# Low parts of weights made by an accumulating load, and four of eight row pairs as seven products, in the last stage of a decoder trunk

## The chip, the cores and the metric

The kernel runs on one core of one Trainium2 chip. The metric is the device time of one execution in microseconds (us). The core has a matrix engine (TensorE, PE in the profile), an elementwise vector engine (VectorE, DVE), an activation engine (ScalarE, ACT), GpSimd (POOL) and SyncE (SP), which here issues all the transfers of the kernel before. Sixteen DMA engines carry the transfers.

## The reference

The program is a decoder trunk of two layers on 256 tokens of width 2048, all in float32. Layer 0 mixes tokens by retention, layer 1 by a gated short convolution; each layer ends with a SwiGLU feed-forward part of inner width 5632, and a final RMS norm closes the trunk. What the change touches is the feed-forward part of layer 1 and the norm behind it:

```python
def swiglu(h, w_in, w_out):
    a, b = jnp.split(h @ w_in, 2, axis=-1)
    return (jax.nn.silu(a) * b) @ w_out
...
        h = (rms_norm(x, norm2_g[i]) * (1.0 + sc2) + sh2).astype(x.dtype)
        x = (x + g2 * swiglu(h, ffn_w_in[i], ffn_w_out[i])).astype(x.dtype)
    return rms_norm(x, final_g).astype(x.dtype)
```

## The kernel before, in words

**Products in two parts.** Each float32 operand is held as a high part, rounded to the matrix engine's float32r type, and a low part, what is left (`lo = raw - hi`). A product of two operands is three matmuls: high by high, high by low, low by high (`thrice`, L460 to L462). The second of the three is the first that needs the low part of the weights.

**Weights.** All weights lie in one array `w_all` in the order of their use, in blocks of 128 x 2048 (1 MB). SP loads a block into a `raw` buffer (three of them, L372). A block is cut into pieces of 1024 columns, or 512. For each piece ACT makes `hi` (L402) and DVE makes `lo` (L405). There are four `hi` and four `lo` buffers (`PART_BUFS`), used in rotation: a piece can be written only when PE is done with the piece four places ahead of it. In the last stage three pieces are prepared ahead of the one in use.

**The last stage.** It is the feed-forward part of layer 1, in two halves (20 and 24 tiles of the inner width). Its first matrix is worked off in ten groups (4 in the first half, 6 in the second), each for four inner tiles; a group goes over eight blocks, 0 to 7, of one pair of row tiles each. The second matrix follows each half in two groups, four in all, of 10 or 12 pairs; the last of them ends with six tiles of rows taken column by column.

**Common blocks and Sevens.** A common block has two pieces, here called b.0 and b.1 for block b, each of four products: 24 matmuls of 512 columns. For some pairs (`IN_SEVEN` of the first matrix, `OUT_SEVEN` of the second) the 2 x 2 blocks of tokens, rows and columns are multiplied with seven products in place of eight (a Strassen-Winograd scheme, class `Seven`): 21 matmuls. Such a block has four pieces, b.2 to b.5, of two, two, two and one product. DVE works more for it: the differences of weight blocks (L391, 1024 columns, into one buffer shown as `x`, since it lies in an old part of x), two further ones in place in `raw` (L395 and L397, 512 columns each), and the low parts of 3.5 times 1024 columns. In place of a common block's two low parts these are four instructions of 1024 columns and three of 512. The sums of tokens that the scheme needs on the other side are made once for the first matrix (`made_in_sums`) and per pair for the second (`tokens_sums_of`, L1142 to L1145).

**At the end of a group.** When the last Seven of a group is done, four banks are combined (`mixed_sums`: ACT's copy L1240, then DVE's L1241 to L1244), and after block 7 the sums are added (L1315, DVE), followed by silu (L1319, ACT) and a product (L1320, DVE). The transposes of this result back to rows (`turned`: PE L1329, ACT L1332 and L1333, DVE L1334) are taken up two blocks into the next group (`TURNS_AT`).

**What sets the order.** PE's order is that of the code. The orders of ACT, DVE, POOL and SP are set at build time by a scheduler, and each engine works through its own list strictly in order: an instruction that waits holds up all behind it.

Of the kernel before, what the change touches and what calls it, by code (L numbers as in the profile page):

```python
# [10 lines left out]
F32 = mybir.dt.float32  # L11
F32R = mybir.dt.float32r
I32 = mybir.dt.int32
AF = mybir.ActivationFunctionType
ALU = mybir.AluOpType
PSUM = bass.MemoryType.PSUM

P = 128
# [14 lines left out]
HALF = 1024  # L33
# [4 lines left out]
LEAD = 6  # L38
ROOTS_AT, SPREAD_AT = 1, 3
TAIL_ROWS = 6  # L40
IN_SEVEN, OUT_SEVEN, TURNS_AT, BESIDE_CB, BESIDE_SUMS = (3, 5), (2, 4, 6), 2, 40, 48
LAST_TILES = 20, 24
STORE_AT, LOAD_AT = 0, 2
LEAD_RET, LEAD_CONV, LEAD_FFN = 6, 4, 2
# [97 lines left out]
class Seven:  # L142
# [6 lines left out]
    n = 2 * DV // P  # L149
# [12 lines left out]
def in_pairs(cols, rows, sevens):  # L162

    return [Seven(cols, r) if i in sevens else Group(cols, DV, ks=r) for i, r in rows]
# [13 lines left out]
def last_out(part):  # L178

    first, n = part * LAST_TILES[0], LAST_TILES[part]  # L180
    order = list(range(n // 2))
    if not part:
        a, b = order[-2:]
        order = order[:5] + [a, order[6], b, order[5], order[7]]
    rows = [(i, [first + 2 * i, first + 2 * i + 1]) for i in order]
    out = []
    for c in range(0, D, 2 * DV):
        cols, rest = [c, c + DV], 0
        if part and c + 2 * DV == D:
            rest = TAIL_ROWS // 2  # L190
        out.append(in_pairs(cols, rows[: len(rows) - rest], OUT_SEVEN))
        if rest:
            out[-1] += [Group([col], DV, ks=[k for _, r in rows[-rest:] for k in r]) for col in cols]
    return out
# [62 lines left out]
def trunk(ctx: ExitStack, tc: tile.TileContext, x_in, c_in, pos_in, w_mod, cols_in, gain_in, tab_in, w_all, out):  # L257
    nc = tc.nc
# [11 lines left out]
    def tmp(tag, shape=(P, S), dtype=F32, pool=work, bufs=None):  # L270
        return pool.tile(list(shape), dtype, tag=tag, name=name(tag), bufs=bufs)
# [11 lines left out]
    cols = const.tile([P, n_cols], F32, tag="cols", name="cols")  # L283
# [78 lines left out]
    in_seven, n = set(), 0  # L362
    for g in groups:
        if isinstance(g, Seven):
            in_seven.add(n // CHUNK)
        n += g.n * P * len(g.ks)

    pieces = [(i, p) for i in range(w_all.shape[0]) for p in ((2, 3, 4, 5) if i in in_seven else (0, 1))]

    def fetch():  # L370
        raw = wpool.tile([P, CHUNK], F32, tag="raw", name=name("raw"), bufs=RAW_BUFS)
# [4 lines left out]
    def prepare(between=None):  # L376
        if prepared[0] == len(pieces):
            return
        _, piece = pieces[prepared[0]]
        prepared[0] += 1  # L380
        if piece in (0, 2):
            if not fetched:
                fetch()
            raws[:] = [fetched.pop(0)]
            while first <= units[0] < early and len(fetched) < RAW_BUFS - 1 and n_fetched[0] < w_all.shape[0]:
                fetch()
        whole = raws[0]
        b = [whole[:, i : i + DV] for i in range(0, CHUNK, DV)]
        raw = whole[:, :HALF] if piece in (0, 4) else whole[:, HALF:]
        if piece == 2:  # L390
            nc.vector.tensor_tensor(differences, whole[:, DV : 3 * DV], whole[:, : 2 * DV], op=ALU.subtract)  # L391
        elif piece == 3:
            raw = differences
        elif piece == 4:
            nc.vector.tensor_tensor(b[1], b[2], differences[:, :DV], op=ALU.subtract)  # L395
        elif piece == 5:
            nc.vector.tensor_tensor(b[3], b[3], b[1], op=ALU.subtract)  # L397
            raw = b[3]
        width = raw.shape[1]
        hi = wpool.tile([P, HALF], F32R, tag="hi", name=name("hi"))[:, :width]  # L400
        lo = wpool.tile([P, HALF], F32R, tag="lo", name=name("lo"))[:, :width]
        nc.scalar.copy(hi, raw)  # L402
        if between:
            between()
        nc.vector.tensor_tensor(lo, raw, hi.bitcast(F32), op=ALU.subtract)  # L405
        ready.append((hi, lo, width))

    prepared, ahead_now = [0], [AHEAD]
# [270 lines left out]
    with ExitStack() as inner:  # L679
# [64 lines left out]
        with tc.tile_pool(name="start", bufs=1) as sp:  # L744
# [132 lines left out]
            due, step = [], [0.0]  # L877
# [245 lines left out]
    def turn(t, c):  # L1123
# [8 lines left out]
    needed(1, GT2)  # L1132
    in_cb = const.tile([P, D], F32R, tag="cb", name="in_cb")
    tokens_sums = [
        v.rearrange("p (i n) -> p i n", i=2) for v in (in_cb[:, : 6 * P], in_cb[:, 6 * P : 12 * P])
    ] + [mpool.tile([P, 2, 3 * P], F32R, tag="sums_of_tokens", name="sums_of_tokens")]

    def tokens_sums_of(a11, a21, a12, a22, third, others):

# [11 lines left out]
    def parts(both):  # L1151

        return [both[:, i, t * P : (t + 1) * P] for i in range(2) for t in range(2)]

    in_sums = {}

    def made_in_sums():

        tmp("beside_sums", (P, BESIDE_SUMS), bufs=1)
        for i in IN_SEVEN:  # L1160
            both = tmp("u512", (P, 2, S), pool=mpool, bufs=3)
            for n in range(2):
                k = 2 * i + n
                high, low = [h[k].bitcast(F32)[:, v, :] for v in range(2)]
                nc.vector.tensor_tensor(both[:, n, :], high, low, op=ALU.add)
            tag = "low" if in_sums else "u"
            in_sums[i] = [tmp(tag, (P, 2, P), F32R, bufs=3) for _ in range(3)]
            tokens_sums_of(*parts(both), h[2 * i][:, :, P:], in_sums[i])

    def three(v):  # L1170
        return [v[:, :, n * P : (n + 1) * P] for n in range(3)]

    turns = [lambda t=t, c=c: turn(t, c) for c in range(4) for t in range(2)]

# [136 lines left out]
    def last_input(groups, pairs, seven):  # L1311

        ours, extra = gathered(groups, h, 0, in_sums)
        for (t, j), pt in ours.items():
            nc.vector.tensor_tensor(extra[t, j], pt, extra[t, j], op=ALU.add)  # L1315
        ms = []
        for t in range(2):
            m = extra[t, 0]
            nc.scalar.activation(m, m, AF.Silu)  # L1319
            nc.vector.tensor_tensor(m, m, extra[t, 1], op=ALU.mult)  # L1320
            ms.append(m)

        def turned():
            for n, (dst, of) in enumerate(zip(pairs, seven)):
                pt = bank()
                for i in range(2):
                    for t, m in enumerate(ms):
                        c = slice((2 * n + i) * P, (2 * n + i + 1) * P)
                        nc.tensor.transpose(pt[:, i, t * P : (t + 1) * P], m[:, c], ident)  # L1329
                if of is not None:  # L1330
                    both = tmp("u512", (P, 2, S), pool=mpool, bufs=3)
                    nc.scalar.copy(both, pt)  # L1332
                nc.scalar.copy(dst[:, :, 0, :], pt)  # L1333
                nc.vector.tensor_tensor(dst[:, :, 1, :], pt, dst[:, :, 0, :].bitcast(F32), op=ALU.subtract)  # L1334
                if of is not None:
                    tokens_sums_of(*parts(both), dst[:, 0, :, P:], [of])

        waiting.append(turned)

    def last_output(part, c, groups, act, base):  # L1340

        final = part and c

        def beside(i):
            if not part and not c and i == STORE_AT:
                gate_stored()
            if not part and not c and i == LOAD_AT:
                spread()
            if part and not c and i == LOAD_AT:
                last_gain = hpool.tile([P, D], F32, tag="h", name="last_gain")  # L1350
                nc.sync.dma_start(last_gain, gain_in.broadcast_to([P, D]))
                gain_of.extend(at(last_gain, v) for v in range(4))

        def mixed(extra):
            for (t, j), v in extra.items():
                gated(t, c + j, v, 0)

        sums = {i: three(v) for i, v in zip(OUT_SEVEN, tokens_sums)}
        ours, extra = gathered(groups, act, base, sums, beside, mixed if final else None)
        if final:  # L1360
            return
        for (t, j), pt in ours.items():
            nc.vector.tensor_tensor(extra[t, j], pt, extra[t, j], op=ALU.add)
        for (t, j), v in extra.items():
            gated(t, c + j, v, MOD_PRIO)
            if part:
                xs, n = at(xt[t], c + j), c + j
                nc.scalar.activation(v, xs, AF.Square, accum_out=total[:, t, n : n + 1])
                nc.vector.tensor_tensor(xs, xs, gain_of[n], op=ALU.mult)
# [16 lines left out]
    for part in range(2):  # L1386
        n = LAST_TILES[part] // 2
        mid = mids(LAST_TILES[part]) if part else first_mid
        if not part:
            first_rows(mid[-2:])  # L1390
            made_in_sums()
            ahead_now[0] = AHEAD + 1
        for i, groups in enumerate(LAST_IN[part]):
            seven = [tokens_sums[OUT_SEVEN.index(q)] if q in OUT_SEVEN else None for q in (2 * i, 2 * i + 1)]
            last_input(groups, mid[2 * i : 2 * i + 2], seven)
        act = [mid[k // 2][:, k % 2] for k in range(2 * n)]
        for c, groups in enumerate(LAST_OUT[part]):
            last_output(part, 2 * c, groups, act, part * LAST_TILES[0])
# [37 lines left out]
```

## Time and profile before

| | |
|---|---|
| time, median of three runs | 2597.03 us (2595.98 to 2597.09) |
| the profiled execution | 2600.71 us, of which the span is 2598.8 us |
| PE busy | 2567.0 us, 99% of the span |
| DVE busy | 2157.4 us, 83% |
| ACT busy | 1289.4 us, 50% |
| POOL busy | 125.7 us, 5%; in the last stage next to nothing |
| loads of weights, in the whole program | 456 of 1 MB |
| mean DMA rate | 265 GB/s |
| granted TensorE clock | 0.999 |

Busy time on PE counts each matmul until its end, and matmuls overlap: one of 512 columns is listed with 390 ns, while the next starts about 227 ns after it. So the pitch from start to start is what a matmul costs on a PE that never waits. DVE's and ACT's instructions overlap a little in the same manner. "Idle before" with an arrow names what an engine waited for just before an instruction.

### The profile page before, as it was taken

The page shows a single profiled execution, that of the slowest core. Times are in us where ns is not written, and L with a number is a line of the kernel's source. Part 1 is how long each engine was busy: PE and PEld are TensorE (multiplying, and loading weights), DVE is VectorE, ACT ScalarE, POOL GpSimd, SP SyncE. Part 2 cuts the span into 40 slices and gives each one's busy share as a digit, 9 for nine tenths or more (in the row PEclk, how much of TensorE's full clock was granted, in tenths as well). Part 3 has the DMA queues.
Part 4 walks back from the last instruction along what each step waited for, and adds up shares of the span by engine and source line. Part 5 has one row for each costly group of instructions (what it writes and reads, how often), then busy time and mean ns, then how long its engine had stood idle before and what let it go on. Part 6 is the DMA issues. An engine that isn't in the chain of part 4 may idle for free.

```text
span 2598.8 us, 36365 instructions
## 1 busy us (share of the span) xinstructions
PE 2567.0 (99%) x14211; PEld 2241.0 (86%) x14211; DVE 2157.4 (83%) x2702; ACT 1289.4 (50%) x1768; POOL 125.7 (5%) x232
## 2 busy tenths in 40 slices
PE   7999999999999999999999999999999999999998
PEld 6898889888889888888888898888998888888886
DVE  7988978887698887777777889988988888888877
ACT  5544543444456454334444454444565554555554
POOL 0000000110000000100001001000000000000000
PEclk9999999999999999999999999999999999999999
DMA  9975668877676888787778868877845565554653
GB/s 399 387 290 221 255 246 300 299 261 276 244 284 247 330 325 305 298 299 302 294 284 296 299 237 313 326 290 277 305 171 204 190 217 203 184 207 182 221 200 146
DMA packets 96686, 689.55 MB, mean 265 GB/s; under 512 B 10737, under 2 KB 12161, under 8 KB 13441
## 3 DMA queue, kind: packets, MB, share of 16 engines
q1 hardware_dynamic: 96514, 687.23, 71.1%
q8 instruction: 111, 1.82, 0.3%
q14 instruction: 61, 0.50, 0.1%
HBM read 685.08 MB, written 2.11 MB: 264 GB/s over the span
## 4 chain that ended last, share of the span: by engine, by line
PE 84%; DVE 7%; DMA 5%; issue 2%; ACT 1%; ACTq 0%; POOLq 0%; POOL 0%; DVEq 0%; SPq 0%
PE bank L447 25%; PE bank L450 14%; PE bank L461 12%; PE bank L460 12%; PE bank L462 12%; DMA raw<-w_all 4%; DVE lo L405 3%; DMA raw<-w_mod 2%; PE bank L496 2%; PE bank L495 1%; PE bank L494 1%; PE bank L627 1%; PE bank L629 1%; PE bank L628 1%; DVE raw L755 1%
## 5 line engine op out<-in xcount | busy, mean ns | idle before, releaser
L402 ACT CAST hi<-raw 128x1024 fp32r<-128x1024 f32 (+1 forms) x944 | 973.1, 1039 | 1037.0 <-PE bank L462 385.6
L405 DVE TENSOR_TENSOR lo<-raw,hi 128x1024 fp32r<-128x1024 f32 (+1 forms) x944 | 1129.9, 1203 | 347.4 <-ACT hi L402 340.0
L447 PE MATMUL bank<-h,hi 128*128 128x512 f32 x2016 | 699.2, 390 | 0.0
L450 PE MATMUL bank<-h,lo 128*128 128x256 f32 x2016 | 568.4, 282 | 0.0
L447 PEld LDWEIGHTS bank<-h,hi 128*128 128x128 f32 x2016 | 378.3, 188 | 79.2
L460 PE MATMUL bank<-hi,h 128*128 128x512 f32 x1072 | 420.1, 392 | 1.8 <-DVE rm L739 1.8
L461 PE MATMUL bank<-lo,h 128*128 128x512 f32 x1072 | 418.3, 390 | 0.7 <-DVE lo L405 0.7
L462 PE MATMUL bank<-hi,h 128*128 128x512 f32 x1072 | 417.6, 390 | 0.0
L318 DVE SCALAR_TENSOR_TENSOR raw<-raw,cb 128x2048 f32<-128x2048 f32 x160 | 365.6, 2285 | 23.2 <-DMA raw<-w_mod 22.9
L450 PEld LDWEIGHTS bank<-h,lo 128*128 128x128 f32 x2016 | 381.0, 189 | 0.0
L447 PE MATMUL bank<-mid,hi 128*128 128x512 f32 x922 | 319.8, 390 | 0.0
L450 PE MATMUL bank<-mid,lo 128*128 128x256 f32 x922 | 260.1, 282 | 0.4 <-DVE lo L405 0.4
L462 PEld LDWEIGHTS bank<-hi,h 128*128 128x128 f32 x1072 | 201.4, 188 | 42.6
L460 PEld LDWEIGHTS bank<-hi,h 128*128 128x128 f32 x1072 | 201.8, 188 | 41.8 <-DVE rm L739 2.4
L461 PEld LDWEIGHTS bank<-lo,h 128*128 128x128 f32 x1072 | 201.9, 188 | 39.9 <-DVE lo L405 1.1
L447 PEld LDWEIGHTS bank<-mid,hi 128*128 128x128 f32 x922 | 173.0, 188 | 36.2
L450 PEld LDWEIGHTS bank<-mid,lo 128*128 128x128 f32 x922 | 174.3, 189 | 0.7 <-DVE lo L405 0.7
L447 PE MATMUL bank<-rm,hi 128*128 128x512 f32 x496 | 172.6, 390 | 0.0
L496 PE MATMUL bank<-h,lo 128*128 128x256 f32 x512 | 146.2, 286 | 5.2 <-DVE lo L405 5.2
L494 PE MATMUL bank<-h,hi 128*128 128x256 f32 x512 | 145.6, 284 | 3.2 <-ACT h L783 3.2
L495 PE MATMUL bank<-h,hi 128*128 128x256 f32 x512 | 145.6, 284 | 0.7 <-DVE h L784 0.7
L450 PE MATMUL bank<-rm,lo 128*128 128x256 f32 x496 | 139.9, 282 | 0.0
(248 smaller groups left out, 3092.4 us busy)
## 6 DMA issues: line engine op xcount, KB each, us to landing
raw<-w_all SPq DMA_DIRECT2D x456, 1024.0 KB, 4.9
raw<-w_mod SPq DMA_DIRECT2D x192, 1024.0 KB, 5.3
x<-x_in SPq DMA_DIRECT2D x4, 512.0 KB, 5.5
out<-xt SPq DMA_DIRECT2D x4, 512.0 KB, 3.0
decay<-tab_in SPq DMA_DIRECT2D x8, 128.0 KB, 2.7
x<-gate_row SPq DMA_DIRECT2D x2, 512.0 KB, 4.4
last_gain<-gain_in SPq DMA_DIRECT2D x1, 1024.0 KB, 4.6
cols<-cols_in SPq DMA_DIRECT2D x1, 152.0 KB, 8.5
```

Source lines behind the costliest of these rows:

```text
L318: nc.vector.scalar_tensor_tensor(raw, raw, 1.0, cb, op0=ALU.mult, op1=ALU.mult, accum_out=total)
L402: nc.scalar.copy(hi, raw)
L405: nc.vector.tensor_tensor(lo, raw, hi.bitcast(F32), op=ALU.subtract)
L447: nc.tensor.matmul(pt, hi, h, start=fresh and k == g.ks[0], stop=False, skip_group_check=True)
L450: nc.tensor.matmul(pt[:, 1, :], lo, h[:, 0, :], start=False, stop=last and k == g.ks[-1], skip_group_check=True)
L460: nc.tensor.matmul(o, hi, w_hi, start=first, stop=False)
L461: nc.tensor.matmul(o, hi, w_lo, start=False, stop=False)
L462: nc.tensor.matmul(o, lo, w_hi, start=False, stop=last)
L494: nc.tensor.matmul(pt, hi, h[:, 0, :], start=first, stop=False, skip_group_check=True)
L495: nc.tensor.matmul(pt, hi, h[:, 1, :], start=False, stop=False, skip_group_check=True)
L496: nc.tensor.matmul(pt, lo, h[:, 0, :], start=False, stop=last, skip_group_check=True)
L627: nc.tensor.matmul(pt, hi, high, start=k == 0, stop=False, skip_group_check=True)
```

## The change

There are two parts. `IN_SEVEN` goes from two pairs (3 and 5) to four neighbouring ones (3, 4, 5 and 6), so that in each of the ten groups of the first matrix four blocks of eight are Sevens. The sums of tokens for the two further pairs are made at the start of the stage and lie in small buffers that were in use before; `OUT_SEVEN` is written per half, with the same values.

And in the last stage, from its third block on, the low part of a common piece is no longer made by DVE: ACT writes minus the high part into `lo`, and a load issued on POOL's queue adds the same 128 x 1024 numbers of `w_all` to it on arrival. Excepted is the first piece of a common block that follows a Seven; that one, and all pieces of Sevens, stay with DVE. 118 pieces are made by such loads.

```diff
-IN_SEVEN, OUT_SEVEN, TURNS_AT, BESIDE_CB, BESIDE_SUMS = (3, 5), (2, 4, 6), 2, 40, 48
+IN_SEVEN, OUT_SEVEN, TURNS_AT, BESIDE_CB, BESIDE_SUMS = (3, 4, 5, 6), ((2, 4, 6), (2, 4, 6)), 2, 40, 48
...
+    last_block = min(in_seven) - IN_SEVEN[0]
     pieces = [(i, p) for i in range(w_all.shape[0]) for p in ((2, 3, 4, 5) if i in in_seven else (0, 1))]
+
+    def low_by_dma(block, piece):
+
+        if piece > 1 or block < last_block + 2:
+            return False
+        return piece == 1 or block - 1 not in in_seven
...
-        nc.vector.tensor_tensor(lo, raw, hi.bitcast(F32), op=ALU.subtract)
+        if low_by_dma(block, piece):
+            nc.scalar.mul(lo, hi.bitcast(F32), -1.0)
+            nc.gpsimd.dma_start(lo, w_all[block, :, piece * HALF : (piece + 1) * HALF], accum_op=ALU.add)
+        else:
+            nc.vector.tensor_tensor(lo, raw, hi.bitcast(F32), op=ALU.subtract)
...
+        for tag, n in (("u", 3), ("low", 3), ("sum", 4)):
+            single_sums.extend(tmp(tag, (P, 2, P), F32R, bufs=n) for _ in range(n))
         for i in IN_SEVEN:
...
-            tag = "low" if in_sums else "u"
-            in_sums[i] = [tmp(tag, (P, 2, P), F32R, bufs=3) for _ in range(3)]
+            in_sums[i] = [single_sums.pop() for _ in range(3)]
```

Some lines move by the edit. In the kernel after it, ACT's cast is L409 (L402 before), DVE's low part L416 (L405), the differences L398, L402 and L404 (L391, L395, L397), the copy of `mixed_sums` L1255 (L1240), the silu L1334 (L1319); ACT's minus the high part is L413 and POOL's load L414.

More of the change, by code (lines that the diff above doesn't have):

```diff
@@ L190, in last_out @@
             rest = TAIL_ROWS // 2
-        out.append(in_pairs(cols, rows[: len(rows) - rest], OUT_SEVEN))
+        out.append(in_pairs(cols, rows[: len(rows) - rest], OUT_SEVEN[part]))
         if rest:
@@ L378, in prepare @@
             return
-        _, piece = pieces[prepared[0]]
+        block, piece = pieces[prepared[0]]
         prepared[0] += 1
@@ L1134, in trunk @@
     tokens_sums = [
-        v.rearrange("p (i n) -> p i n", i=2) for v in (in_cb[:, : 6 * P], in_cb[:, 6 * P : 12 * P])
-    ] + [mpool.tile([P, 2, 3 * P], F32R, tag="sums_of_tokens", name="sums_of_tokens")]
+        [v.rearrange("p (i n) -> p i n", i=2)] for v in (in_cb[:, : 6 * P], in_cb[:, 6 * P : 12 * P])
+    ] + [[mpool.tile([P, 2, 3 * P], F32R, tag="sums_of_tokens", name="sums_of_tokens")]]
+    single_sums = [in_cb[:, n * P : (n + 2) * P].rearrange("p (i n) -> p i n", i=2) for n in (12, 14)]
     def tokens_sums_of(a11, a21, a12, a22, third, others):
@@ L1165, in made_in_sums @@
                 nc.vector.tensor_tensor(both[:, n, :], high, low, op=ALU.add)
-            tag = "low" if in_sums else "u"
-            in_sums[i] = [tmp(tag, (P, 2, P), F32R, bufs=3) for _ in range(3)]
+            in_sums[i] = [single_sums.pop() for _ in range(3)]
             tokens_sums_of(*parts(both), h[2 * i][:, :, P:], in_sums[i])
+        if single_sums[2:]:
+            tokens_sums.append([single_sums.pop() for _ in range(3)])
     def three(v):
-        return [v[:, :, n * P : (n + 1) * P] for n in range(3)]
+        return [v[0][:, :, n * P : (n + 1) * P] for n in range(3)] if len(v) == 1 else v
     turns = [lambda t=t, c=c: turn(t, c) for c in range(4) for t in range(2)]
@@ L1335, in turned @@
                 if of is not None:
-                    tokens_sums_of(*parts(both), dst[:, 0, :, P:], [of])
+                    tokens_sums_of(*parts(both), dst[:, 0, :, P:], of)
         waiting.append(turned)
@@ L1356, in mixed @@
                 gated(t, c + j, v, 0)
-        sums = {i: three(v) for i, v in zip(OUT_SEVEN, tokens_sums)}
+        sums = {i: three(v) for i, v in zip(OUT_SEVEN[part], tokens_sums)}
         ours, extra = gathered(groups, act, base, sums, beside, mixed if final else None)
@@ L1393, in trunk @@
         for i, groups in enumerate(LAST_IN[part]):
-            seven = [tokens_sums[OUT_SEVEN.index(q)] if q in OUT_SEVEN else None for q in (2 * i, 2 * i + 1)]
+            due = OUT_SEVEN[part]
+            seven = [tokens_sums[due.index(q)] if q in due else None for q in (2 * i, 2 * i + 1)]
             last_input(groups, mid[2 * i : 2 * i + 2], seven)
```

## The prediction

> **What bounds the kernel now.** I read the engine table of the page first, then the waits of PE, then the last stage alone: by stretches, by groups of instructions, by timeline.
>
> ```profile
> PE 2567.0 (99%) x14211; PEld 2241.0 (86%) x14211; DVE 2157.4 (83%) x2702; ACT 1289.4 (50%) x1768; POOL 125.7 (5%) x232
> ```
>
> ```profile
> PE bank L461 <- DVE lo L405: 2.4, 4, 0.8
> ...
> PE bank L450 <- DVE lo L405: 0.4, 1, 0.4
> ```
>
> PE hardly waits: for low parts in the lines of the last stage (L460 to L462) 2.4 us in the whole program. The next rows are two stretches of that stage (columns: busy us of PE, PEld, DVE, ACT and POOL, granted clock, DMA share, GB/s).
>
> ```profile
> 2000.00:2100.00 100.00, 100.00 (x451) 82.86 (x450) 84.89 (x104) 54.56 (x65) 0.00 (x0) 1.00 0.55 202
> 2200.00:2300.00 100.00, 100.00 (x451) 82.99 (x450) 83.74 (x94) 50.12 (x54) 0.00 (x0) 1.00 0.55 198
> ```
>
> PE is full at a full clock, DVE follows with 84%. So a matmul less is time won, provided that DVE and the loads still deliver each piece in time; the lead is only three pieces. Its measures come from one timeline, of PE, then ACT, then DVE:
>
> ```profile
> 2238.05 0.39 PE L462 MATMUL bank<-hi,h 128*128 128x512 f32 x1
> ...
> 2255.73 0.39 PE L462 MATMUL bank<-hi,h 128*128 128x512 f32 x1
> 2255.96 1.03 PE L1329 MATMUL bank<-tab,x 128*128 128x128 f32 x8
> 2256.75 0.48 PE L460 MATMUL bank<-hi,h 128*128 128x512 f32 x1
> ```
>
> ```profile
> 2256.20 1.05 ACT L402 CAST hi<-x 128x1024 fp32r<-128x1024 f32 x1 [1.67 <-PE bank L462]
> ```
>
> ```profile
> 2257.28 1.23 DVE L405 TENSOR_TENSOR lo<-x,hi 128x1024 fp32r<-128x1024 f32 x1 [0.77 <-ACT hi L402]
> ```
>
> Between the first two PE rows lie 78 matmuls: 17.68 / 78 = 0.2267 us each. A product is 0.68 us, a common piece 2.72, a common block 5.44, a Seven 21 x 0.2267 = 4.76. A buffer that PE leaves at 2255.96 gets its cast 0.24 us later; the cast takes 1.05, and the low part follows at once.
>
> **The change: what goes.** The built order of PE has 13,952 rows where it had 14,012: ten groups, two more Sevens each, three matmuls fewer in each. 60 x 0.2267 = **13.6 us less**, 1.36 per group. DVE also loses 118 low parts, but it is not the bound in common blocks; that gains nothing by itself.
>
> **DVE in four neighbouring Sevens.** The pitch of DVE, undisturbed:
>
> ```profile
> 2215.31 1.22 DVE L405 TENSOR_TENSOR lo<-x,hi 128x1024 fp32r<-128x1024 f32 x1
> 2216.45 0.68 DVE L1204 TENSOR_TENSOR xt<-xt,x 128x512 f32<-128x512 f32 x1
> 2217.05 1.22 DVE L391 TENSOR_TENSOR x<-raw 128x1024 f32<-128x1024 f32 x1
> 2218.18 1.22 DVE L405 TENSOR_TENSOR lo<-raw,hi 128x1024 fp32r<-128x1024 f32 x1
> 2219.32 0.69 DVE L395 TENSOR_TENSOR raw<-raw,x 128x512 f32<-128x512 f32 x1
> ```
>
> 1.14 us for 1024 columns, 0.60 for 512. A Seven costs DVE 4 x 1.14 + 3 x 0.60 = 6.36 us, against 4.76 on PE; a common block 2.28 against 5.44. Before, DVE's list in the first matrix has a common block (L405 twice in a row, `raw_22052`, block 4) between the pieces of the Sevens 3 and 5 (`raw_22074` is 5):
>
> ```order
> L405 TENSOR_TENSOR lo_22043<-raw_21960,hi_22042 128x512 [waits Activation_49]
> L395 TENSOR_TENSOR raw_22074<-raw_22074,x_75 128x512 [waits DVE_49]
> L405 TENSOR_TENSOR lo_22055<-raw_22052,hi_22054 128x1024 [waits DMAHW7_49,Activation_49]
> L405 TENSOR_TENSOR lo_22065<-raw_22052,hi_22064 128x1024 [waits Activation_49]
> L405 TENSOR_TENSOR lo_22078<-raw_22074,hi_22077 128x1024 [waits Activation_49]
> L405 TENSOR_TENSOR lo_22085<-x_75,hi_22084 128x1024 [waits Activation_49]
> L397 TENSOR_TENSOR raw_22074<-raw_22074 128x512 [waits DVE_49]
> ```
>
> 6.36 + 2.28 + 6.36 = 15.0 against 14.96 of PE: balanced. In the changed order of DVE the same place holds Seven behind Seven (`raw_21597` is block 5, `raw_21639` block 6):
>
> ```order
> L398 TENSOR_TENSOR x_75<-raw_21597 128x1024 [waits DMAHW0_49,DVE_49]
> L416 TENSOR_TENSOR lo_21601<-raw_21597,hi_21600 128x1024 [waits Activation_49]
> L402 TENSOR_TENSOR raw_21597<-raw_21597,x_75 128x512 [waits DMAHW5_49,DVE_49]
> L416 TENSOR_TENSOR lo_21611<-x_75,hi_21610 128x1024 [waits Activation_49]
> L404 TENSOR_TENSOR raw_21597<-raw_21597 128x512 [waits DVE_49]
> L416 TENSOR_TENSOR lo_21622<-raw_21597,hi_21621 128x1024 [waits Activation_49]
> L416 TENSOR_TENSOR lo_21630<-raw_21597,hi_21629 128x512 [waits Activation_49]
> L398 TENSOR_TENSOR x_75<-raw_21639 128x1024 [waits DMAHW1_49]
> L416 TENSOR_TENSOR lo_21643<-raw_21639,hi_21642 128x1024 [waits Activation_49]
> ```
>
> The relief in the common blocks moved nothing forward: a low part can't be made before its buffer is left. Let PE begin block 3 at 0. Piece 4.2 uses the buffer that 3.2 leaves at 1.36; cast 1.60 to 2.65, low part 2.68 to 3.82. From there DVE goes down its list without a pause. Ends by pitch, and in brackets when PE wants the piece (its second matmul): 4.3 5.57 (6.35), 5.2 9.59 (9.75), 5.3 11.33 (11.11), 5.4 13.07 (12.47), 6.2 15.95 (14.51), 6.3 17.69 (15.87), 6.4 19.43 (17.23). With 0.1 for the end of an instruction and the semaphore, PE is 2.3 us late: **10 x 2.3 = +23 us**. Ends: nothing, if more is done ahead than the buffers seem to allow, and 6.4 x 10 (the whole excess, 25.4 less 19.0 per group).
>
> **The accumulating loads.** Per piece ACT gets a second pass (`mul`, taken as 1.05 like the cast), then POOL issues the load, then it must land. ACT has room: 4 x 1.05 in a common block of 5.44. POOL's list in this stage is the 118 loads in the order of use, with two sums of the final norm between them that wait for squares of ACT which stand ahead of the next `mul` anyway; so a load that waits for its `mul` holds up only later ones. SP's list has the same loads as before. Who waits is PE, with everything behind the piece. ACT's list at the turn from a group to the next, before (`raw_22150` is block 7, `raw_22182` the next block 0):
>
> ```order
> L402 CAST hi_22152<-raw_22150 128x1024 [waits DMAHW2_49,DVE_49,PE_49]
> L402 CAST hi_22166<-raw_22150 128x1024 [waits DVE_49,PE_49]
> L402 CAST hi_22184<-raw_22182 128x1024 [waits DMAHW3_49,DVE_49,PE_49]
> L402 CAST hi_22200<-raw_22182 128x1024 [waits DVE_49,PE_49]
> L402 CAST hi_22218<-raw_22216 128x1024 [waits DMAHW4_49,DVE_49,PE_49]
> ```
>
> and after (`raw_22399` is block 7, `raw_22422` the next block 0):
>
> ```order
> L409 CAST hi_22401<-raw_22399 128x1024 [waits DMAHW2_49,PE_49,Activation_49]
> L409 CAST hi_22411<-raw_22399 128x1024 [waits PE_49,Activation_49]
> L409 CAST hi_22424<-raw_22422 128x1024 [waits DMAHW3_49,DVE_49,PE_49]
> L413 ACTIVATE lo_22412<-hi_22411 128x1024 [waits DMASW6_49,Activation_49]
> L413 ACTIVATE lo_22425<-hi_22424 128x1024 [waits DMASW7_49,Activation_49]
> ```
>
> The `mul` of piece 7.1 stands behind the cast of the next 0.0, whose buffer PE leaves with 6.4, 0.68 before block 7. With block 7 at 0: cast from -0.44, `mul` until 1.66. PE wants 7.1 at 2.72 + 0.23 = 2.95. So from the end of `mul` to PE's matmul there are 1.2 us (0.1 for the semaphore). Call the landing time L: PE stands L - 1.2 there, in each of ten groups. In the second matrix 3.1 behind a Seven has `mul` right behind its cast, which waits for 2.3: it ends 5.06 after the Seven's start, and 7.71 is wanted: L - 2.55, eight times. Behind the last Seven ACT's copy (L1255) comes in between, 0.5 more: L - 2.05, four times. Other pieces have 4.4 to 6 us.
>
> L has no row, for no load of before adds. The nearest rows, in the last stage and on the page (last column: us from issue to landing):
>
> ```profile
> raw<-w_all SPq DMA_DIRECT2D x106, 1024.0 KB, 4.8
> x<-gate_row SPq DMA_DIRECT2D x2, 512.0 KB, 4.4
> ```
>
> ```profile
> out<-xt SPq DMA_DIRECT2D x4, 512.0 KB, 3.0
> decay<-tab_in SPq DMA_DIRECT2D x8, 128.0 KB, 2.7
> ```
>
> I take **L = 4.4**, the row of the same size in the same stage; as an ACT-to-PE figure it leaves out POOL's own issue time. Below, L = 2.7: even 128 KB took that. Above, 7.4: 4.4 and another pass of 3.0 for reading `lo` and writing it back. Then: 10 x 3.2 = **32**; 8 x 1.85 + 4 x 2.35 = **24**. In the first matrix, piece 1.1 of the next group stands on ACT behind two silus (L1319, now L1334), which wait for sums of DVE behind PE's delayed block 7. These and the copy, mean ns as the second number:
>
> ```profile
> L1319 ACT ACTIVATE x<-x 128x512 f32<-128x512 f32 x20 | 12.7, 633 | 3.6 <-DVE x L1315 3.6
> ...
> L1240 ACT COPY x<-bank 128x512 f32<-128x512 f32 x13 | 7.5, 576 | 0.0
> ```
>
> PE leaves 7.1 at 5.44 + 3.2 = 8.64; DVE's first two sums (0.60 each) end at 9.4 and 10.0, the silus at 10.7, cast and `mul` at 12.75, landing 17.15; wanted 13.6 + 3.2 + 0.23 = 17.0. Late by 0.15: **1.5** (at L = 2.7 nothing; at 7.4 the same steps give 3.2 each).
>
> The Trainium skill (DMA: Bandwidth & Descriptors, Anatomy of one DMA) gives a load from GpSimd 2.0 us and its bytes at 436 GB/s, an estimated 3.2 us for 512 KB, and by that the sum below would be 41 us, not 69; no run here shows such a load yet, and the page's figure is for one that does not add.
>
> **The sums of tokens** for two more pairs, once: two additions of 0.35 and eight instructions of 0.20 each,
>
> ```profile
> 1921.87 0.28 DVE L1142 TENSOR_TENSOR u<-u 128x128 f32<-128x128 f32 x1
> 1922.08 0.28 DVE L1143 TENSOR_TENSOR u<-u 128x128 f32<-128x128 f32 x1
> ...
> 1924.57 0.42 DVE L506 TENSOR_TENSOR sum<-bank,low 128x256 f32<-128x256 f32 x1
> 1924.91 0.42 DVE L1165 TENSOR_TENSOR u<-h 128x256 f32<-128x256 f32 x1
> ```
>
> 2 x 2.3 = 4.6 us of DVE: 0 to 4.6 on PE, taken as **2**.
>
> **Sum**: -13.6 + 23 + 32 + 1.5 + 24 + 2 = +69 us. The profiled execution took 2600.7 (3.7 above the median of 2597.0), so 2670 in its terms, **2666** against the median.
>
> **The rivals.**
> *The matmuls' gain arrives* (faster). If the loads land within the 1.2 us that the shortest lead leaves, and DVE keeps up in the Sevens, only the 13.6 us are left: 2597 - 13.6 = 2583. Places: 7.1, and 6.4. It decides as soon as all stalls stay under 13.6, that is 0.6 per place (22 places). For it: DVE's total for a group doesn't rise (seven low parts out, 8; two Sevens in for common blocks, 8.2), and POOL is idle. Against it: 2.7 us is the shortest load in the rows. 0.11.
> *DVE alone.* Loads in time, Sevens short: -13.6 + 23 + 2 = +11, 2608. Against: the same row. 0.05.
> *The DMA engines fill up.* A group moves 8 x 1.05 + 7 x 0.52 = 12.1 MB in 40 us, 302 GB/s, 393 if reading `lo` counts; the most in a slice of the page is 399:
>
> ```profile
> DMA  9975668877676888787778868877845565554653
> GB/s 399 387 290 221 255 246 300 299 261 276 244 284 247 330 325 305 298 299 302 294 284 296 299 237 313 326 290 277 305 171 204 190 217 203 184 207 182 221 200 146
> ```
>
> Then a load queues behind a whole raw load, L = 4.8 + 4.8 = 9.6: 10 x (8.4 + 5.4) + 8 x 7.05 + 4 x 7.55 + 23 + 2 - 13.6 = +236, 2833. For it: raw loads are issued at the same turn. Against: the mean stays under the limit while reading `lo` is not counted. 0.07.
>
> **How the numbers follow.** My forecast, Sevens short and loads late with L of 2.7 to 7.4: 0.74. Its ends: at 2.7 with half of the 23, -13.6 + 11.5 + 15 + 4 = +17, 2614; at 7.4, -13.6 + 23 + 62 + 32 + 60 + 4 = +167, 2764. About 0.03 is left for balances within 0.2%, about what a measurement can tell from no change. The range takes in DVE alone: 2607 to 2764. Faster 0.11, same 0.03, slower 0.86.
>
> **What would show it.** Right: PE waits at L472 for the loads of L414, most at 7.1, and at L472 for DVE's L416 in blocks 5 and 6; the loads land in 3 to 7 us; about 60 matmuls fewer; the second matrix longer too. Wrong: PE still full in the first matrix; loads landing near 1 us, or over 8; waits for L414 at all common pieces alike, which would be the DMA engines' rate.

## The result, and the profile after

The changed kernel takes 2881.57 us (median of four runs, 2876.22 to 2885.53) against 2597.06: **1.109 times as long**, 95% interval 1.108 to 1.111. The forecast was 2666 with a range to 2764; the direction was right and the size was not.

The page of the changed kernel: the engines (answering to the first row of the prediction), the 40 slices, the queues and the transfers.

```profile
span 2873.3 us, 36874 instructions
...
PE 2642.8 (92%) x14151; PEld 2260.4 (79%) x14151; DVE 2115.0 (74%) x2704; ACT 1436.5 (50%) x1934; POOL 227.0 (8%) x350
...
PEclk9999999999999999999999999999998999999888
DMA  9966777776868877887876888766676677766686
...
q1 hardware_dynamic: 96514, 687.23, 64.3%
q0 software_dynamic: 16992, 61.87, 11.3%
...
raw<-w_all SPq DMA_DIRECT2D x456, 1024.0 KB, 5.1
raw<-w_mod SPq DMA_DIRECT2D x192, 1024.0 KB, 5.4
lo<-w_all POOLq DMA_DIRECT2D x118, 512.0 KB, 10.1
```

The last row is the number that the prediction lacked: an adding load lands 10.1 us after its issue (median of 118), not 4.4. The queue rows point at a reason, which the experiments below test. The third column is the share of all 16 engines' span: q1 takes 0.643 x 2873.3 / 648 = 2.85 us of all engines for 1 MB (648 loads of that size make up nearly all of it), q0 0.113 x 2873.3 / 118 = 2.75 us for 512 KB. Byte for byte an adding load occupies the engines nearly twice as long.

PE's waits in the whole program, and the two stretches shown before:

```profile
PE bank L472 <- DMA lo<-w_all: 193.8, 57, 9.0
...
PE bank L472 <- DVE lo L416: 5.2, 10, 0.5
```

```profile
2000.00:2100.00 100.00, 77.04 (x308) 58.52 (x308) 62.76 (x79) 56.66 (x66) 9.60 (x11) 0.91 0.68 199
2200.00:2300.00 100.00, 74.40 (x278) 58.16 (x279) 39.45 (x47) 47.00 (x49) 13.09 (x15) 0.88 0.69 199
```

PE is busy for 74 to 77 us of 100 that were full, and its granted clock is 0.88 to 0.91 (third column from the end). The span of the profiled execution grew by 274.5 us. PE's idle time (span less busy) grew from 31.8 to 230.5, by 199, nearly all of it waits for L414's loads. PE's busy time grew by 76, although 60 matmuls of 13.6 us are gone: the matmuls that are left take 89 us more. The largest part of that is a lower clock: without the last stretch, at the program's end, the trace's clock records hold 174 us at half the clock, and PE is busy in 117 of them, so half of these, 58 us by estimate, is lost. Another 16 us come with the further Sevens alone (their run below has the same matmuls and 2569.7 us of PE busy); the last 15 are not traced.

Where PE waits is known by piece, since POOL's loads are issued in the order of use. The ten loads of piece 7.1 cost 85 us, and the twelve of the second piece behind a Seven in the second matrix 52: these 22 hold 138 us of the 194. Each of these waits is the landing time less the lead, and the leads are within 0.2 us of those that the prediction gave: in the median 8.6 us at 7.1 (landing 9.9, lead 1.2 to 1.3) and 4.3 us in the second matrix (landing 6.6, lead 1.9 to 2.5). Piece 1.1 of the next group adds 16 us, all others 40. One of the ten waits at 7.1:

```profile
2153.87 0.79 PE L472 MATMUL bank<-lo,h 128*128 128x512 f32 x1 [8.65 <-DMA lo<-w_all]
```

How the clock falls is seen where PE waits (start, duration, the wait in brackets):

```profile
2215.40 0.39 PE L471 MATMUL bank<-hi,mid 128*128 128x512 f32 x1
2220.40 0.80 PE L472 MATMUL bank<-lo,mid 128*128 128x512 f32 x1 [4.61 <-DMA lo<-w_all]
2220.99 0.63 PE L473 MATMUL bank<-hi,mid 128*128 128x512 f32 x1
2221.42 0.63 PE L471 MATMUL bank<-hi,mid 128*128 128x512 f32 x1
...
2224.83 0.47 PE L473 MATMUL bank<-hi,mid 128*128 128x512 f32 x1
2225.14 0.39 PE L471 MATMUL bank<-hi,mid 128*128 128x512 f32 x1
...
2235.56 0.50 PE L472 MATMUL bank<-lo,mid 128*128 128x512 f32 x1 [1.46 <-DMA lo<-w_all]
2235.90 0.40 PE L473 MATMUL bank<-hi,mid 128*128 128x512 f32 x1
2236.14 0.40 PE L471 MATMUL bank<-hi,mid 128*128 128x512 f32 x1
```

After a wait of 4.61 us the next matmuls start 0.43 us apart, until 4.4 us later the pitch is back at 0.23. After a wait of 1.46 us it is 0.34 once and 0.24 from there.

### The profile page after: what moved, and what is told of

Same layout as the page of the kernel before. It is cut to its first block, busy times and chain, and to the rows that moved or that the text cites. A ratio compares the mean times of both kernels' runs of the same rounds, so it can differ in the third digit from the quotient of the medians.

```text
span 2873.3 us, 36874 instructions
## 1 busy us (share of the span) xinstructions
PE 2642.8 (92%) x14151; PEld 2260.4 (79%) x14151; DVE 2115.0 (74%) x2704; ACT 1436.5 (50%) x1934; POOL 227.0 (8%) x350
## 4 chain that ended last, share of the span: by engine, by line
PE 69%; DMA 16%; DVE 8%; issue 5%; ACT 2%; POOL 0%; POOLq 0%; ACTq 0%; DVEq 0%; SPq 0%
PE bank L458 25%; PE bank L461 13%; DMA lo<-w_all 13%; PE bank L472 8%; PE bank L473 7%; PE bank L471 6%; DVE lo L416 4%; PE bank L507 2%; PE bank L506 2%; PE bank L505 2%; DMA raw<-w_all 2%; DMA raw<-w_mod 1%; ACT hi L409 1%; PE bank L638 1%; PE bank L640 1%
## 5 line engine op out<-in xcount | busy, mean ns | idle before, releaser
L409 ACT CAST hi<-raw 128x1024 fp32r<-128x1024 f32 (+1 forms) x964 | 978.8, 1027 | 1031.7 <-PE bank L473 384.9
L416 DVE TENSOR_TENSOR lo<-raw,hi 128x1024 fp32r<-128x1024 f32 (+1 forms) x846 | 999.5, 1190 | 429.0 <-ACT hi L409 424.8
L472 PE MATMUL bank<-lo,h 128*128 128x512 f32 x992 | 404.4, 408 | 119.4 <-DMA lo<-w_all 117.7
L471 PE MATMUL bank<-hi,h 128*128 128x512 f32 x992 | 397.9, 401 | 1.9 <-DVE rm L750 1.9
L473 PE MATMUL bank<-hi,h 128*128 128x512 f32 x992 | 396.4, 400 | 0.0
L472 PEld LDWEIGHTS bank<-lo,h 128*128 128x128 f32 x992 | 192.8, 194 | 177.1 <-DMA lo<-w_all 130.3
L471 PEld LDWEIGHTS bank<-hi,h 128*128 128x128 f32 x992 | 192.3, 194 | 41.7 <-DVE rm L750 2.5
L473 PEld LDWEIGHTS bank<-hi,h 128*128 128x128 f32 x992 | 192.9, 194 | 40.1
L472 PE MATMUL bank<-lo,mid 128*128 128x512 f32 x304 | 135.3, 445 | 76.5 <-DMA lo<-w_all 76.1
L414 POOL DMA_DIRECT2D lo<-w_all x118 | 103.2, 874 | 852.2 <-ACT lo L413 788.6
L505 PE MATMUL bank<-h,hi 128*128 128x256 f32 x512 | 145.7, 285 | 3.2 <-ACT h L794 3.2
## 6 DMA issues: line engine op xcount, KB each, us to landing
lo<-w_all POOLq DMA_DIRECT2D x118, 512.0 KB, 10.1
```

Of the source, the lines that this page charges most:

```text
L414: nc.gpsimd.dma_start(lo, w_all[block, :, piece * HALF : (piece + 1) * HALF], accum_op=ALU.add)
L471: nc.tensor.matmul(o, hi, w_hi, start=first, stop=False)
L472: nc.tensor.matmul(o, hi, w_lo, start=False, stop=False)
L473: nc.tensor.matmul(o, lo, w_hi, start=False, stop=last)
L505: nc.tensor.matmul(pt, hi, h[:, 0, :], start=first, stop=False, skip_group_check=True)
```

## The experiments

Times are compared with the kernel before on the same chip, 2597 to 2598.5 us. The variants with loads were timed once each, the one on the clock twice; only differences of more than 10 us are read from the single times.

**Each part alone.** First the Sevens without the loads:

```diff
-        return piece == 1 or block - 1 not in in_seven
+        return False
```

> Only the first part of the change: four neighbouring Sevens, all low parts by DVE. Theory A (the adding loads occupy the DMA engines twice as long per byte as a plain load, queue up at the turn of a group, and PE waits and then runs at a lower granted clock): the loads are the loss, so this kernel lies between 2597 - 13.6 + 23 = 2607 us (the DVE term of the prediction) and 2597 - 13.6 + 10 x 6.4 = 2647 us, with waits of PE for DVE only and a granted clock near 1. Theory B (the fixed path through POOL is slow, whatever is added): the same here. Theory C (DVE in four neighbouring Sevens is the loss): above 2800 us.

2608.94 us against 2596.97, ratio 1.0045 (1.0028 to 1.0062): +12.0 us, where the prediction's rival "DVE alone" had +11. Theory C falls: four neighbouring Sevens make DVE the bound, but that is 12 us of 284. The two stretches shown in the prediction, and PE's wait for DVE's low parts:

```profile
2000.00:2100.00 100.00, 97.92 (x423) 76.81 (x424) 98.89 (x123) 61.70 (x75) 0.00 (x0) 1.00 0.54 200
2200.00:2300.00 100.00, 98.30 (x424) 77.71 (x423) 94.59 (x110) 55.59 (x61) 0.00 (x0) 1.00 0.49 184
```

```profile
PE bank L472 <- DVE lo L416: 5.6, 11, 0.5
```

The clock is 1.00, and DVE is busy for 95 to 99 us of 100 where it was 84 to 85. The wait row shows little of the delay, because a matmul is listed as busy for 0.16 us after the next could start. From start to start, matmuls that begin late lose 25.3 us in the last stage, against 3.6 in the kernel before: 22 us more, where the prediction had 23.

Then the loads without the further Sevens:

```diff
-IN_SEVEN, ... = (3, 4, 5, 6), ...
+IN_SEVEN, ... = (3, 5), ...
```

> Only the second part: adding loads, with Sevens at 3 and 5 as before; there are then 148 such loads, 10 per group of the first matrix in place of 7. Theory A: a group needs 10 x 2.75 + 8 x 2.85 = 50 us of all DMA engines and has 41 us on PE, so at least 2597 + 10 x 9 = 2687, and with the queueing and the clock that the changed kernel showed about 2900 us; the loads land later than 10 us. Theory B: each load lands in about 10 us as before, 148 in place of 118, about 2950 us. Theory C: about 2597 us.

2929.46 us, +332, with 148 loads. Loads land in 9.2 us, PE waits 226.7 us for them, the clock is 0.962:

```profile
PE bank L472 <- DMA lo<-w_all: 226.7, 84, 6.8
```

Per load that is 2.2 us, as in the changed kernel (2881.6 less 2608.9 is 272; 272 / 118 = 2.3). The loads are the loss, whatever the Sevens do. That they land no later than there goes against A's wording; A and B are not yet told apart.

**What in a load takes long.** The same loads without adding, and adding loads of half the size:

```diff
-            nc.gpsimd.dma_start(lo, w_all[block, :, piece * HALF : (piece + 1) * HALF], accum_op=ALU.add)
+            nc.gpsimd.dma_start(lo, w_all[block, :, piece * HALF : (piece + 1) * HALF])
```

> The changed kernel with the same 118 loads on POOL's queue, but they overwrite the low part and add nothing, so the low parts of these pieces are the weights themselves. Theory A: the load takes the engines half as long (1.4 us per 512 KB in place of 2.75), lands in 4 to 5.5 us, and the time is 2660 to 2720 us. Theory B: it lands in about 10 us still, 2880 us. Theory C: 2880 us.

2773.34 us; landing 7.0 us.

```diff
-            nc.gpsimd.dma_start(lo, w_all[block, :, piece * HALF : (piece + 1) * HALF], accum_op=ALU.add)
+            nc.gpsimd.dma_start(lo[:, :DV], w_all[block, :, piece * HALF : piece * HALF + DV], accum_op=ALU.add)
```

> The changed kernel with adding loads of half the width, 128 x 512 numbers each; the other half of these low parts stays minus the high part. Theory A: half the engine time, lands in 5 to 6 us, 2680 to 2740 us. Theory B: a load lands in over 9 us still, above 2850 us. Theory C: 2880 us.

2791.12 us; landing 7.1 us. The rows of the two, first of the overwriting loads, then of the halved ones:

```profile
q0 software_dynamic: 16992, 61.87, 6.8%
...
lo<-w_all POOLq DMA_DIRECT2D x118, 512.0 KB, 7.0
```

```profile
q0 software_dynamic: 16992, 30.94, 6.6%
...
lo<-w_all POOLq DMA_DIRECT2D x118, 256.0 KB, 7.1
```

By the spans of these runs (2771.6 and 2789.4) a load takes 1.60 and 1.56 us of the engines: overwriting 512 KB costs what adding 256 KB costs. So the landing time follows the engines' time, as theory A has it, and B's constant 10 us is excluded. But both runs are slower than A's numbers (2660 to 2720 and 2680 to 2740): an overwriting load of 512 KB on POOL's queue still lands in 7.0 us where SP's row of that size had 4.4 in the kernel before. Beside these loads SP's own row is no faster:

```profile
x<-gate_row SPq DMA_DIRECT2D x2, 512.0 KB, 7.3
```

Adding is worth 108 us of the 284, not all.

The source was moved from HBM to the `raw` buffer, which holds the same numbers:

```diff
-            nc.gpsimd.dma_start(lo, w_all[block, :, piece * HALF : (piece + 1) * HALF], accum_op=ALU.add)
+            nc.gpsimd.dma_start(lo, raw, accum_op=ALU.add)
```

> The changed kernel with the adding loads taken from the raw buffer in SBUF, where the same numbers lie already, in place of w_all in HBM. If the second reading (of the low part) is what doubles the engines' time, it stays at 2.6 to 2.9 us per 512 KB, landing near 10 us and the time 2850 us or more, since the raw buffer is also held until the load has landed. If reading HBM a second time were the cost: half of it, landing 5 to 7 us, below 2780 us.

2818.65 us, between the two cases. 0.115 x 2816.3 / 118 = 2.74 us of the engines per load, as with HBM, so the second reading of the weights from HBM is not what takes the engines' time; with the 1.60 of the overwriting load beside it, it is the adding. Landing went from 10.1 to 8.9:

```profile
q0 software_dynamic: 16992, 61.87, 11.5%
...
lo<-raw POOLq DMA_DIRECT2D x118, 512.0 KB, 8.9
```

**Short lead or too many?** The prediction had PE wait at the 22 pieces with the shortest lead. Without the loads of just those:

```diff
-        return piece == 1 or block - 1 not in in_seven
+        return block - 1 not in in_seven
```

> The changed kernel without the 22 loads that have the shortest lead (the second piece behind a Seven: 7.1 in the first matrix, 3.1 and its like in the second); these low parts go back to DVE, 96 loads are left. Theory A1 (as the prediction had it: PE waits where the lead is short): 2609 us as with the Sevens alone, plus at most 20. Theory A2 (an adding load lands in 6 us alone and in 10 in a row, more than the 4.4 to 6 us that all other pieces have, and two of them and a raw load need 8.4 us of the DMA engines per common block of 5.44): still above 2700 us.

2800.66 us, so A1 falls and A2 holds: 96 loads with the long lead still cost 192 us beyond the 2608.9 of the Sevens alone, 2.0 per load. They land in 10.8 us:

```profile
PE bank L472 <- DMA lo<-w_all: 135.5, 41, 8.0
```

That does not mean that the short leads cost nothing in the changed kernel: they cost 138 us of waits there. Without their loads other pieces wait. Piece 0.0 alone waits 6.2 to 6.8 us in eight of nine groups; landing less wait gives it a lead of 3.5 us, less than the 4.4 to 6 of the prediction, where PE has stood still at 7.1 before.

And at most one load per common block, 28 in all:

```diff
-        return piece == 1 or block - 1 not in in_seven
+        rel = block - last_block
+        spot = rel % 8 if rel < 32 else (rel - 52) % 8 if 52 <= rel < 100 else 8
+        return piece == 0 and spot < 3
```

> The changed kernel with 28 adding loads only: the first pieces of blocks 0, 1 and 2 in the first matrix, at most one per common block, none in the second matrix; the rest by DVE. Theory A2: the DMA engines have room (3 x 2.8 + 8 x 2.9 = 32 us in a group of 40), loads land in about 6 us, the lead is about that: 2609 us plus 0 to 40, clock above 0.99. If the landing time is 10 us whatever stands beside it: 10 x 3 x 4 = 120 us more, 2730.

2667.89 us, 59 above the Sevens alone: over the 40 that A2 allowed, and half of the other case's 120. Landing 7.3 us (5.4 to 10.3), with the engines at 60%. Of the 37.7 us that PE waits (the first row below), 33.8 are again at piece 0.0, with its lead of 3.5 us; the 19 loads of 1.0 and 2.0, with leads of 5.2 us and more, cost 3.9. So a thinly spread load is late where the lead is short, and "about 6" was wrong for 0.0.

> The 28 loads of the run with few loads, but overwriting in place of adding (these low parts are then the weights themselves). Theory A2 (an adding load alone takes 5.4 to 7.3 us because of its adding): landing 4 to 5.5 us, within the lead, so 2609 to 2635 us in place of 2668. If the path through POOL is slow by itself: landing 7 us, 2668 us.

With those 28 overwriting in place of adding (the edit of the overwriting run): 2646.12 us, landing 6.1 (3.7 to 7.4). This is over the 2635 that theory A allowed and under the 2668 of the other; both have a part. Waits of PE, adding, then overwriting:

```profile
PE bank L474 <- DMA lo<-w_all: 37.7, 12, 5.5
```

```profile
PE bank L474 <- DMA lo<-w_all: 22.0, 8, 3.3
```

The traces of these two runs also tell what a load waits for. Here the 28 loads of each are sorted by the loads of SP and POOL that are issued and not yet landed when they are issued (median landing time in us, number of loads):

| others under way | overwriting | adding |
|---|---|---|
| none | 4.1 (5) | 5.4 (5) |
| one | 4.2 (6) | 5.5 (4) |
| two | 6.3 (11) | 7.4 (11) |
| three | 6.8 (6) | 9.6 (8) |

In the run with 118 overwriting loads, where more of them follow at once, those issued with none under way land in 5.6 us (5). In the changed kernel the landing goes on to 11.4 with four (22 loads) and 12.9 with five (10). The raw loads pay too: in that kernel one that is issued with two or more of POOL's under way lands in 9.7 us (26 loads), one with none in 4.9 (71).

**The clock.** Twelve repetitions of a matmul were put ahead of the one that waits, at the 22 places of shortest lead:

```diff
...
         nc.tensor.matmul(o, hi, w_hi, start=first, stop=False)
+        if warm[0]:
+            warm[0] = False
+            for _ in range(12):
+                nc.tensor.matmul(o, hi, w_hi, start=False, stop=False)
```

> The changed kernel with 12 matmuls too many (a repetition of the high-by-high one, 2.7 us at the full clock) ahead of the waiting one at each of the 22 places with the shortest lead: 264 matmuls, 60 us of work, which fall into waits of 4 to 9 us; the result holds these repetitions. Theory K (PE's idling takes the granted clock down, and that costs matmul time beside the waits): the clock rises above 0.969 and the time does not rise by the 60 us: it is 2840 to 2885 us. Without an effect of idling on the clock: the extra work is hidden in the waits and the time stays at 2881, or it rises by up to 60 where the wait is shorter; the clock stays at 0.97.

2870.96 us (two runs, 2870.68 and 2871.23) against 2881.57 (2876.22 to 2885.53): 264 matmuls more, 60 us of work at the full clock, and 10.6 us less time in the median; the slower of these two is 5.0 us under the fastest of the four. The clock went from 0.969 to 0.980. PE's waits for the loads fell from 193.8 to 142.8:

```profile
PE bank L478 <- DMA lo<-w_all: 142.8, 58, 6.4
```

The time at half the clock fell from 174 to 113 us, and PE's busy time rose by 46.8 us where the added work is 60. The extra work lies inside waits (at the 22 places they fell from 138 to 80 us) and keeps the clock up behind them. So PE's idling takes the clock down, and that costs time beside the waits themselves; only these 22 places have the extra matmuls.

**A version that is a little faster.** Three Sevens per group with a common block between each two, and no loads:

```diff
-IN_SEVEN, ... = (3, 4, 5, 6), ...
+IN_SEVEN, ... = (2, 4, 6), ...
...
-        return piece == 1 or block - 1 not in in_seven
+        return False
```

> No adding loads, and three Sevens per group with a common block between each two (2, 4 and 6) in place of four neighbours. By DVE's pitch: 6.36 for a Seven and 2.28 for a common block are 8.64 us against 10.2 of PE, so DVE keeps up; PE has 10 x 3 = 30 matmuls fewer than the kernel before: 2597 - 6.8 = 2590 us. If DVE's other work in the group (8 us) can't be fitted in: up to 2605.

2593.05 us against 2598.13 of the kernel before on that chip, ratio 0.998 (0.997 to 0.999): 5.1 us of the 6.8 that the matmuls are worth. PE's only wait for a low part of DVE's in the lines of the last stage:

```profile
PE bank L472 <- DVE lo L416: 0.5, 1, 0.5
```

With a fourth Seven in two groups of the second matrix:

```diff
-..., ((2, 4, 6), (2, 4, 6)), ...
+..., ((2, 4, 6), (2, 4, 6, 8)), ...
```

> No adding loads, Sevens at 2, 4 and 6 in the first matrix, and a fourth Seven (pair 8) in both groups of the second matrix of the second half: 36 matmuls fewer than the kernel before, 6 fewer than the run with Sevens at 2, 4 and 6 alone. By PE's pitch 1.4 us less than that: 2591.7 us, about 2588.9 to 2593 by the best case of 2597 - 8.2. If the further sums of tokens are late for DVE: up to 2597.

2593.87 us against 2598.46, ratio 0.9986 (0.9977 to 0.9995). The further 1.4 us are not seen; the two versions can't be told apart. Both beat the kernel before and the changed one.

## Why the prediction was wrong

- **13.6 us from 60 matmuls fewer, and DVE short in four neighbouring Sevens (+23, with 2 for the sums of tokens)**: held. The Sevens alone cost 12.0 us where these terms give 11, and the late starts that came with them are 22 us where the term had 23. The pitches of 1.14 and 0.60 us, and DVE going down its list without a pause, were the right reading.
- **L = 4.4**, the landing time of an adding load: the step that failed. It was read from SP's row for 512 KB in the same stage. That row is two loads that each read one row of 1024 numbers for all 128 partitions (L1207 in the kernel after), add nothing and met none of POOL's loads; beside these loads the same row measured 7.9 in the changed kernel. The adding load measured 10.1 (5.6 to 13.2), from 2.75 us of all engines per load and from the other loads under way. The prediction's own upper end, 7.4, came from one more pass of 3.0 us; its upper rival, a load behind a whole raw load, had 9.6. No row of the kernel before bounded an adding load from above, and the range treated 7.4 as if one did. The Trainium skill's formula (DMA: Bandwidth & Descriptors, Anatomy of one DMA), by estimate 3.2 us for 512 KB, was lower still: the fastest overwriting loads took 3.7 and 3.8 us here, the adding ones from HBM 5.3 at best.
- **Where PE waits** was right: most at 7.1, by landing time less lead, with the leads as forecast. The terms 32, 24 and 1.5 measured 85, 52 and 16, because L was 9.9 at 7.1 and 6.6 in the second matrix. One L for all places was wrong too. With L = 10.1 throughout, the same terms give -13.6 + 23 + 2 + 10 x (8.9 + 5.9) + 8 x 7.55 + 4 x 8.05 = +252 us, against +284 measured. That nearness is partly luck: those three terms are then 241 us where 154 were measured, and the 40 us of other waits and the clock are not in it.
- **"Other pieces have 4.4 to 6 us"** was put at no cost. In the changed kernel their waits are 40 us. With the 22 shortest leads out of the way the loss was still 202.5 us, because a landing time of 10 is over all these leads, and 0.0 then has only 3.5.
- **"The DMA engines fill up", 0.07**: this rival came nearest in time (2833), and its L of 9.6 is close to the 9.9 of 7.1; its chance was too low. Loads do wait beside other loads, as the table shows. But the engines were 72% busy in the last stage, not full, and PE's waits were not alike at all common pieces, which the prediction had named as the sign of the engines' rate. The working held the hint: 393 of at most 399 GB/s if the reading of `lo` counts. That the reading is what makes adding dearer is not shown; shown is that adding takes 2.75 us of the engines and overwriting 1.60. In a common block two adding loads and a raw load need 2 x 2.75 + 2.85 = 8.35 us of all engines, and PE takes 5.44.
- **The clock** was no term. The rows of before showed it full because PE never waited; waits were priced at their own length. It cost by estimate 58 us more.
- "The matmuls' gain arrives", 0.11: excluded by the same landing times.

In the run with 28, an overwriting load on POOL's queue that is issued with nothing else under way lands in 4.1 us (3.7 to 4.3), no later than SP's row of that size in the kernel before (3.8 and 5.0). So POOL's own path isn't needed to explain the 6.1 and 7.0. What stays open is how the loads share the engines: the table sorts loads that also stand at different places of the program, and no run changed only the number of loads beside one.

## What to carry to other kernels

When work moves from a busy engine to a load, count the time that the load takes of all DMA engines together, with that of the loads beside it in the same few microseconds, before looking at bytes; an adding load counts nearly twice (2.75 us for 512 KB, where a raw load takes 2.85 for 1 MB). Compare its landing time with the shortest lead in buffers, and where no row shows such a load, leave the upper end open or measure it first. On a full PE a wait of some microseconds costs its length and then the slow matmuls behind it, and a helper engine that is busy 84% on average can be short where its heavy blocks stand side by side: three of them spread (2, 4, 6) gained 5 us where four neighbours lost 12.

## What the runs showed of the hardware

- An adding load of 512 KB takes 2.75 us of all 16 DMA engines, an overwriting one 1.60, a raw load of 1 MB 2.85; from HBM or from SBUF makes no difference to it (2.75 and 2.74).
- In the runs with 28 loads, one of 512 KB on POOL's queue lands in 4.1 us with nothing else under way and in 6.8 with three other loads when it overwrites, in 5.4 and 9.6 when it adds.
- POOL is busy 0.87 us with the issue of an adding load (first rows, the changed kernel) and 0.54 with that of an overwriting one (last row):

```profile
2216.52 1.81 POOL L414 DMA_DIRECT2D lo<-w_all  x2 [1.96 <-ACT lo L413]
2219.49 0.87 POOL L414 DMA_DIRECT2D lo<-w_all  x1 [1.15 <-ACT lo L413]
```

```profile
2254.43 0.54 POOL L414 DMA_DIRECT2D lo<-w_all  x1 [14.89 <-ACT lo L413]
```

- The matmul pitch doubles behind a wait of 4.6 us, 0.43 in place of 0.23, and is back after 4.4 us; behind a wait of 1.5 us it stays. The Trainium skill (TensorE: Matmul & The Clock Gate, Part 1: The HAM clock gate) states half the clock after an idle window of about 3.4 us, and the full one after such a window of work; the waits shown here agree, and the stretches at half the clock in the changed kernel's trace last 3.4, 6.8 or 10.2 us.
- More matmuls in the waits cost no time: 264 more, and 10.6 us less in the median.
